# SSM scan of a hybrid decoder layer: chunks stored by their place in the block, a third of the group pairs scanned on GpSimd, queues and order of the work around it changed

## The chip, the cores and the metric

One core of one Trainium2 chip. The metric is the device time of one execution in microseconds (us), median of the runs. Engines: PE = TensorE, DVE = VectorE, ACT = ScalarE, POOL = GpSimd, SP = SyncE (DMA queue only). DMAs are issued from the queues of SP (`dma`), ACT (`put`) and POOL (`later`); each queue is taken in order.

## The reference

One layer for 512 prompt tokens and 8 sample tokens (520 columns), float32:

```
x = x + 0.5 * SwiGLU_1(rmsnorm(x))
z = rmsnorm(x) @ w_in            # [u | q | k | v | gate_a | gate_b]: 1024 + 3*768 + 2*1024 columns
h_t = abar * h_{t-1} + bbar u_t  # S5 SSM: 64 groups of 16 channels, 64 complex states each
y   = gelu(Re(C h) + D u);  A = (y * sigmoid(y @ w_glu)) @ w_proj_a
B   = mixed attention of 3 groups x 4 heads, windows 128/512/2048, dilations 1/4/16, then w_proj_b
x = x + (sigmoid(gate_a) * A + sigmoid(gate_b) * B) @ w_out
x = x + 0.5 * SwiGLU_2(rmsnorm(x))
```

Also returned: the last SSM states, the new keys and values, and the samples' caches moved on by one row.

## The kernel before, in words

Every matrix product is "a product" here: one block of 128 output rows by 520 columns, for K = 1024 eight slices of K, each three matmuls (high x high, high x low, low x high part of a split float32) for each of two column halves: 48 matmuls on line 218 (`mm`). Its weight (512 KB) is loaded by SP (L176), its high part is rounded on ACT (L166), its low part is made on DVE (L167); two raw buffers and six half-weight buffers run ahead. Matmuls under `mark` run on PE in program order.

The mixing stage has 42 products of `w_in` in this order: q blocks 0 and 1; the eight u blocks; q and k blocks 2 to 11; six v blocks; sixteen gates; then eight products of `w_glu`. Behind products the function `pace` counts n (n = 1 behind u block 6, 2 behind u block 7, 3 to 12 behind qk blocks 2 to 11, 13 to 18 behind the v blocks, 19 to 34 behind the gates, 35 on behind `w_glu`) and issues shares of the other work: `SC` scan steps per product, and the lists `LV`, `NB`, `AT`, `KS`, `SM`, `YB` name the n behind which a step of another generator goes.

The SSM path:
- each u block is scaled by 1/rms on DVE into `us` (L791, L793: six instructions), stored to DRAM `uD` by SP (L796, four DMAs a block);
- `entry` (from u block m > `ENTER` = 2 on, four pairs of groups a product): loads of `uD` (POOL, L644) and of the entry matrices `pD` (SP, L658), matmuls on L672, ACT copies into the states `XS` (L673). 32 pairs of groups, 128 chunks of four tokens, plus 8 samples;
- `scan` (L680 to L725), in two halves of 16 pairs on DVE: seven wide steps sum blocks of eight chunks, sixteen short steps carry the state over the sixteen blocks, seven wide steps fill the blocks. `advance` (L688) makes four tensor_tensor instructions: t1 = W0*x, t2 = W1*swap(x), t1 += t2, out = add + t1 (L697 to L700). Chunks lie in the order of time, so a wide step reads and writes every eighth element. The halves are interleaved by `scans`;
- `leave` (L751): eight groups of four pairs; loads of `qD` and `uD` (POOL), 24 matmuls (L758 to L760), one ACT copy (L761), and for each two groups eight stores to `yD` by SP (L768);
- `y_block` (L1037): loads from `yD` (POOL), gelu on ACT and DVE, split; the input of `w_glu`.

Beside it: `normal`/`normalise`/`spread` (norms of q and k, rows broadcast from DRAM `hD` by SP, L844), `attention`, `scores` (samples' scores over the cached keys, in the third buffer of the matrices' ring), `samples`.

Of the kernel before, what the change touches and what calls it, by code (L numbers as in the profile page):

```python
# [10 lines left out]
F32 = mybir.dt.float32  # L11
# [38 lines left out]
SM = (31, 31, 36, 39, 39)  # L50
YB = (29, 29, 29, 29, 29, 31, 31, 33)
NL = 12
# [6 lines left out]
def build(tc, A):  # L59
# [57 lines left out]
    # what is issued inside waits for a value of the arithmetic  # L117
# [5 lines left out]
    # the moves spread over the time of the arithmetic  # L123
# [55 lines left out]
    # the first weights come in halves  # L179
# [25 lines left out]
    # the tensor engine takes these in the order given here  # L205
# [37 lines left out]
    class Norm:  # L243
# [26 lines left out]
        # a quarter of the rows on each quadrant of the partitions while 1/rms is made, then all on each,  # L270
        # through DRAM where that is soon enough
# [33 lines left out]
    def ffn(pf, xs, R, X, last_x, filler, first=(), last=False):  # L305
        first = list(first)

        # products whose rows' 1/rms is still being made leave their banks before it is there
# [14 lines left out]
        for pi, (m0, m1) in enumerate(PARTS):  # L323
# [35 lines left out]
    # the tensor engine's clock rises with use, so it is kept busy while the first rows come  # L359
# [17 lines left out]
    # the first two products go along with the rows' arrival  # L377
# [12 lines left out]
    def ssm_build():  # L390
# [13 lines left out]
        # the skip term joins the lag kernels' first block  # L404
# [56 lines left out]
        # input factor (abar - 1) / lambda  # L461
# [47 lines left out]
        # per eight pairs of groups: entry matrices, exit matrices, lag kernels  # L509
# [5 lines left out]
        for qt in range(4):  # L515
# [15 lines left out]
            # two pairs to a transpose  # L531
# [28 lines left out]
            # a pair to each quarter of the columns  # L560
# [40 lines left out]
    # ================= mixing: one projection, then the SSM and the attention =================  # L601
# [15 lines left out]
    # queries and keys: their 1/rms comes in with the norm over each head  # L617
# [16 lines left out]
    NH = NP // 2  # L634
    XS = [smp.tile([128, 2, NH, 145], F32, name=f"XS{h}") for h in range(2)]
    for ri, n in enumerate(("x0_re", "x0_im")):
        for h in range(2):
            dma(XS[h][:, ri, :, 0:8], A[n].rearrange("p (a b) -> p a b", b=8)[:, h * NH:(h + 1) * NH])
    for h in range(2):
        V.memset(XS[h][:, :, :, 8:9], 0.0)  # L640

# [5 lines left out]
    # block-diagonal over a pair of groups: the blocks are loaded, the zeros stay  # L647
# [16 lines left out]
    # what each chunk's input adds to the state behind it  # L664
    def entry():
        for u in range(NP // 4):
            ut, mp = uload(u), mload(pD, u, dma)
            for a in range(4):
# [4 lines left out]
                S.activation(XS[p // NH][:, :, p % NH, 9:145], ps[:, 0:2], AF.Copy)  # L673
# [4 lines left out]
    # the states in front of every chunk, for a half of the pairs: the sums of sixteen blocks of eight chunks,  # L678
    # the states in front of the blocks, then those inside
    def scan(h):  # L680
        X, pr = XS[h], slice(h * NH, (h + 1) * NH)
        sums = smp.tile([128, 2, NH, 16], F32, name="sums", tag="sums", bufs=2)

# [4 lines left out]
        def advance(out, W, x, add):  # L688
            n = 1 if len(x.shape) == 3 else x.shape[3]
            t1, t2 = (tmp(t)[:, 0:2 * NH * n] for t in "ST")  # L690
            w = [c[:, :, pr] for c in W]
            if n == 1:
                t1, t2 = (t.rearrange("p (r a) -> p r a", r=2) for t in (t1, t2))
            else:
                w = [c.unsqueeze(3).broadcast_to([128, 2, NH, n]) for c in w]
                t1, t2 = (t.rearrange("p (r a b) -> p r a b", r=2, b=n) for t in (t1, t2))
            V.tensor_tensor(t1, w[0], x, ALU.mult)  # L697
            V.tensor_tensor(t2, w[1], swap(x), ALU.mult)  # L698
            V.tensor_tensor(t1, t1, t2, ALU.add)  # L699
            V.tensor_tensor(out, add, t1, ALU.add)  # L700

        def at(j):
            return X[:, :, :, 8 + j:8 + j + 121:8]

        for j in range(1, 8):
            advance(sums, W4, sums if j > 1 else at(1), at(1 + j))
            yield
        for b in range(16):
            advance(X[:, :, :, 16 + 8 * b], W32, X[:, :, :, 8 + 8 * b], sums[:, :, :, b])
# [5 lines left out]
        # sample states  # L715
        x0 = [X[:, ri, :, 0:8] for ri in range(2)]
        xn = [X[:, ri, :, 137:145] for ri in range(2)]
        t = tmp("S")[:, 0:8 * NH].rearrange("p (a b) -> p a b", b=8)
        ab = lambda ri: A1[:, ri, pr].unsqueeze(2).broadcast_to([128, NH, 8])
        for o, a, b, op in ((0, 0, 0, ALU.add), (0, 1, 1, ALU.subtract), (1, 0, 1, ALU.add), (1, 1, 0, ALU.add)):  # L720
            V.tensor_tensor(t, ab(a), x0[b], ALU.mult)
            V.tensor_tensor(xn[o], xn[o], t, op)
        for ri in range(2):
            later(A["ostate"][ri][:, pr], X[:, ri, :, 136:145])
        yield  # L725

    # the short steps of one half go along with the wide ones of the other
    def scans():
        lo, hi = scan(0), scan(1)
        for order in ((lo,) * 7, (lo, hi) * 8, (lo, hi) * 7 + (hi,), (lo,), (hi,) * 8):  # L730
# [3 lines left out]

    scanning = scans()
    paced = {"n": 0, "s": 0}
# [13 lines left out]
    # exit from the states, and the products inside a chunk  # L750
    def leave():  # L751
        for u in range(NP // 4):
            mt, ut, ps = mload(qD, u, later), uload(u), big()
            X, p0 = XS[u * 4 // NH], u * 4 % NH
            for a in range(4):
# [17 lines left out]
    # four segments of tokens, the samples' in front of the first and behind the last, zeros elsewhere;  # L773
    # they go to DRAM with segment and channel on the rows, two groups to a pair
# [3 lines left out]
    for m in range(KB):  # L778
        ps = big()
        mm(ps, wnext(), n2.xs, between=entering if m > ENTER else None)  # L780
        u = us.next()
        # the columns' halves of 260 tokens cut the third segment
        for hf, c0, c1 in ((0, 0, 256), (0, 256, 260), (1, 260, 384), (1, 384, 512)):
            o = u[:, c0 // 128:(c1 + 127) // 128, 8 + c0 % 128:8 + (c1 - 1) % 128 + 1]
            src = ps[:, hf, c0 - hf * H:c1 - hf * H]
            r = R2[:, c0:c1]
            if c1 - c0 > 128:
                src, r = (x.rearrange("p (a b) -> p a b", b=128) for x in (src, r))
            else:
                o = o[:, 0]  # L790
            V.tensor_tensor(o, src, r, ALU.mult)  # L791
        for o in (u[:, 0, 0:8], u[:, 3, NC:CW]):
            V.tensor_tensor(o, ps[:, 1, 512 - H:520 - H], R2[:, 512:520], ALU.mult)  # L793
# [6 lines left out]
    # 1/rms of the rows along the partitions, in the order of the tiles and in that of all the rest  # L800
# [553 lines left out]
```

## Time and profile before

| | us |
|---|---|
| runs (3) | 1324.02, 1325.77, 1328.04 |
| median | 1325.77 |
| span of the profiled execution (first to last instruction) | 1323.7 |
| PE busy | 1265.4 (96%) |
| DVE / ACT / POOL busy | 755.1 / 468.4 / 126.7 |
| mean granted clock of PE | 0.981 |

The profiled execution is one of its own; beside the span lies some 2 us to the median of the runs. Times in views are us from the first instruction. A group row of the trace has its count after "x", then busy us and mean ns of one; after the second bar, idle time in front of the group and what ended it. A window row has, after the stretch and its length, the busy us and count of each engine, the granted clock (PEclk), the busy share of the 16 DMA engines and GB/s.

### The profile page before, as it was taken

What the parts mean: (1) busy time and instruction counts of PE and PEld (TensorE: products, weight loads), DVE (VectorE), ACT (ScalarE), POOL (GpSimd) and SP (SyncE); (2) the same over time, 40 slices, a digit from 0 to 9 for tenths busy, and PEclk for the clock granted to TensorE, in tenths of its full rate; (3) what the DMA queues carried; (4) which work ended last, traced back from release to release, by engine and by line L of the source; (5) the groups of instructions that cost most, each with busy time, mean ns of one, the idle gap of its engine ahead of it and who ended that gap; (6) DMA issues with size and microseconds to landing.
All of it is one profiled execution on the core that took longest, in us unless ns stands there. A gap on an engine that the chain in (4) does not pass through costs nothing.

```text
span 1323.7 us, 25773 instructions
## 1 busy us (share of the span) xinstructions
PE 1265.4 (96%) x10575; PEld 1240.9 (94%) x10575; DVE 755.1 (57%) x1468; ACT 468.4 (35%) x873; POOL 126.7 (10%) x211
## 2 busy tenths in 40 slices
PE   8999999999999779997679999999999999999999
PEld 7999999999999778997578899999999999999998
DVE  6794454545564239999724776776554334444442
ACT  5332233223353223342224564444333223322331
POOL 0120010001103001001221120000010001000000
PEclk9999999999999898998789999999999999999999
DMA  6665366456656445227998635546575436533332
GB/s 216 216 212 178 101 228 191 137 168 206 188 175 155 125 125 155 81 70 242 159 160 245 208 124 145 173 153 206 172 252 162 147 93 223 160 96 112 120 100 85
DMA packets 105438, 213.92 MB, mean 162 GB/s; under 512 B 45300, under 2 KB 61200, under 8 KB 104552
## 3 DMA queue, kind: packets, MB, share of 16 engines
q1 hardware_dynamic: 87064, 145.90, 36.4%
q0 software_dynamic: 7248, 60.01, 15.2%
q10 hardware_dynamic: 11008, 6.36, 2.1%
q8 instruction: 83, 1.36, 0.4%
q14 instruction: 35, 0.29, 0.1%
HBM read 188.72 MB, written 68.60 MB: 194 GB/s over the span
## 4 chain that ended last, share of the span: by engine, by line
PE 76%; DMA 11%; DVE 8%; issue 2%; SPq 1%; ACT 1%; POOL 0%; DVEq 0%; ACTq 0%; POOLq 0%
PE bigB L218 33%; PE bigA L218 28%; PE third L218 12%; DMA wr<-in_win 3%; DMA OB<-hD 2%; DVE wl L167 2%; DMA yD<-XS 2%; DMA t_G<-yD 1%; DVE t_T L698 1%; DVE t_S L697 1%; DMA mt<-qkD 1%; DMA uD<-us 1%; DVE XS L700 1%; DVE t_S L699 1%; ACT wh L166 0%
## 5 line engine op out<-in xcount | busy, mean ns | idle before, releaser
L166 ACT ACTIVATE wh<-wr 128x512 fp32r<-128x512 f32 (+2 forms) x412 | 252.7, 617 | 600.0 <-PE bigB L218 226.0
L167 DVE TENSOR_TENSOR wl<-wr,wh 128x512 fp32r<-128x512 f32 (+2 forms) x412 | 276.6, 672 | 279.6 <-ACT wh L166 275.6
L218 PE MATMUL bigB<-xh,wh 128*128 128x260 f32 (+1 forms) x1216 | 252.9, 289 | 0.3 <-ACT ks L568 0.3
L218 PE MATMUL bigB<-xh,wl 128*128 128x260 f32 (+1 forms) x1216 | 251.9, 287 | 0.0
L218 PE MATMUL bigB<-xl,wh 128*128 128x260 f32 (+1 forms) x1216 | 249.1, 286 | 0.0
L218 PEld LDWEIGHTS bigB<-xh,wl 128*128 128x128 f32 x1216 | 191.6, 191 | 2.4 <-issue 2.4
L218 PEld LDWEIGHTS bigB<-xh,wh 128*128 128x128 f32 x1216 | 190.6, 192 | 1.8 <-issue 0.8
L218 PEld LDWEIGHTS bigB<-xl,wh 128*128 128x128 f32 x1216 | 190.4, 191 | 1.1 <-issue 1.1
L218 PE MATMUL bigA<-xh,wh 128*128 128x260 f32 x704 | 143.1, 284 | 2.5 <-ACT xh L254 2.0
L218 PE MATMUL bigA<-xl,wh 128*128 128x260 f32 x704 | 142.5, 284 | 1.0 <-DVE xl L255 0.9
L218 PE MATMUL bigA<-xh,wl 128*128 128x260 f32 x704 | 142.3, 284 | 0.0
L218 PEld LDWEIGHTS bigA<-xh,wh 128*128 128x128 f32 x704 | 109.1, 190 | 4.4 <-ACT xh L254 3.4
L218 PEld LDWEIGHTS bigA<-xl,wh 128*128 128x128 f32 x704 | 108.8, 189 | 1.6 <-DVE xl L255 1.6
L218 PEld LDWEIGHTS bigA<-xh,wl 128*128 128x128 f32 x704 | 109.1, 190 | 0.2 <-DVE wl L167 0.2
L120 POOL COPY pace<-ah 1x1 f32<-1x1 f32 x48 | 36.1, 751 | 758.2 <-ACT ah L298 758.2
L218 PE MATMUL bigA<-ah,wh 128*128 128x260 f32 x352 | 71.4, 284 | 0.0
L218 PE MATMUL bigA<-al,wh 128*128 128x260 f32 x352 | 71.1, 283 | 0.0
L218 PE MATMUL bigA<-ah,wl 128*128 128x260 f32 x352 | 70.6, 282 | 0.0
L218 PE MATMUL third<-xh,wl 128*128 128x260 f32 x288 | 58.2, 283 | 0.0
L218 PE MATMUL third<-xh,wh 128*128 128x260 f32 x288 | 58.0, 282 | 0.0
L218 PE MATMUL third<-xl,wh 128*128 128x260 f32 x288 | 57.8, 282 | 0.0
L218 PEld LDWEIGHTS bigA<-ah,wh 128*128 128x128 f32 x352 | 54.2, 189 | 0.2
(384 smaller groups left out, 2038.7 us busy)
## 6 DMA issues: line engine op xcount, KB each, us to landing
out_okv<-in_kv POOLq DMA_DIRECT2D x32, 1023.5 KB, 6.3
wr<-in_wg SPq DMA_DIRECT2D x43, 512.0 KB
wr<-in_wu SPq DMA_DIRECT2D x43, 512.0 KB
wr<-in_win SPq DMA_DIRECT2D x42, 512.0 KB
wr<-in_wd SPq DMA_DIRECT2D x32, 448.0 KB
wr<-in_wd SPq DMA_DIRECT2D x16, 512.0 KB
out_okv<-in_kv POOLq DMA_DIRECT2D x8, 1022.0 KB, 5.8
ut<-uD POOLq DMA_DIRECT2D x16, 288.0 KB, 5.5
```

What stands on the lines that cost most here:

```text
L120: ins = G.tensor_copy(pace[0:1, 0:1], t[0:1, 0:1])
L166: S.activation(h, raw, AF.Copy)
L167: V.tensor_tensor(l, raw, h, ALU.subtract)
L218: i = T.matmul(ps[:, hf, 0:x.shape[1]], lhsT=a[:, c], rhs=x, start=k == 0 and j == 0, stop=k == n - 1 and j == 2)
L697: V.tensor_tensor(t1, w[0], x, ALU.mult)
L698: V.tensor_tensor(t2, w[1], swap(x), ALU.mult)
L699: V.tensor_tensor(t1, t1, t2, ALU.add)
L700: V.tensor_tensor(out, add, t1, ALU.add)
```

## The change

It keeps a chunk at column 24 + 16*(place in its block of eight) + block, so that a wide scan step works on runs of 16 adjacent elements; the u blocks are written in that order by DVE and put back in the order of time by the ACT copies of `leave` (three in place of one). The pairs are in three parts (16, 8, 8); the first and the third are scanned on DVE, the second on GpSimd. `sums` and temporaries of a scan are held through it. Queues: `us` stores, `yD` stores and `spread` go from SP to POOL, `pD` loads from SP to ACT, the `Rt` columns and the final states from POOL to SP (the states as six DMAs once at the end). `pace` steps, the lists and `NL` are new; exits come at n = 14 to 18 in place of 21 to 26, y blocks at 25 to 30 in place of 29 to 33, scores at 27 to 31 in place of 22 to 28 with buffers of the samples' ring.

```diff
-ENTER = 2
+ENTER = 3
-SC = 1.85
-LV = (21, 22, 22, 24, 25, 25, 26, 26)
-NB = (16, 17, 17, 17, 18, 18, 19, 20, 21, 22, 22, 22, 22)
-AT = (23, 24, 26, 27, 27, 28, 28, 29, 29, 30, 30, 31, 31, 31, 32, 32, 33, 35, 37)
-KS = (22, 23, 23, 24, 26, 26, 27, 28)
-YB = (29, 29, 29, 29, 29, 31, 31, 33)
-NL = 12
+GROUPS = (16, 8, 8)
+SC = 3.0
+SG = 2.3
+LV = (14, 14, 15, 15, 16, 16, 18, 18)
+NB = (15, 15, 16, 16, 17, 17, 18, 18, 19, 19, 20, 20, 21)
+AT = (22, 23, 24, 24, 25, 25, 26, 27, 27, 28, 28, 29, 30, 30, 31, 32, 32, 33, 35)
+KS = (27, 28, 28, 29, 29, 30, 31, 31)
+YB = (25, 25, 26, 26, 27, 28, 29, 30)
+NL = 6
...
-    XS = [smp.tile([128, 2, NH, 145], F32, name=f"XS{h}") for h in range(2)]
+    XS = [smp.tile([128, 2, n, 160], F32, name=f"XS{h}") for h, n in enumerate(GROUPS)]
...
-            ut, mp = uload(u), mload(pD, u, dma)
+            ut, mp = uload(u), mload(pD, u, put)
...
-    def scan(h):
+    def scan(h, E, tags):
...
-            V.tensor_tensor(t1, w[0], x, ALU.mult)
-            V.tensor_tensor(t2, w[1], swap(x), ALU.mult)
-            V.tensor_tensor(t1, t1, t2, ALU.add)
-            V.tensor_tensor(out, add, t1, ALU.add)
+            E.tensor_tensor(t1, w[0], x, ALU.mult)
+            E.tensor_tensor(t2, w[1], swap(x), ALU.mult)
+            E.tensor_tensor(t1, t1, t2, ALU.add)
+            E.tensor_tensor(out, add, t1, ALU.add)
         def at(j):
-            return X[:, :, :, 8 + j:8 + j + 121:8]
+            return X[:, :, :, 8 + 16 * j:24 + 16 * j]
...
-        lo, hi = scan(0), scan(1)
-        for order in ((lo,) * 7, (lo, hi) * 8, (lo, hi) * 7 + (hi,), (lo,), (hi,) * 8):
+        lo, hi = (scan(h, V, [tmp("G"), tmp("S"), tmp("T")]) for h in (0, 2))
+        for order in ((lo,) * 11, (lo, hi) * 12, (hi,) * 11):
...
+    scanning_too = scan(1, G, [room[:, 1792:2048], dist[:, 0:256], dist[:, 256:512]])
...
-        while paced["s"] < paced["n"] * SC:
+        while paced["s"] < (paced["n"] - 1) * SC:
             next(scanning, None)
             paced["s"] += 1
+        while paced["g"] < (paced["n"] - 3) * SG:
+            next(scanning_too, None)
+            paced["g"] += 1
...
-            S.activation(X[:, 0, p0:p0 + 4, 0:NC].rearrange("p (x a) b -> p x a b", x=2),
-                         ps[:, :, 0:2 * NC].rearrange("p x (a b) -> p x a b", b=NC), AF.Copy)
+            for x in range(2):
+                o, r = X[:, 0, p0 + 2 * x:p0 + 2 * x + 2, 0:NC], ps[:, x, 0:2 * NC].rearrange("p (a b) -> p a b", b=NC)
+                S.activation(o[:, :, 8:NC].rearrange("p a (b j) -> p a b j", j=8),
+                             r[:, :, 8:NC].rearrange("p a (j b) -> p a b j", j=8), AF.Copy)
+            S.activation(X[:, 0, p0:p0 + 4, 0:8].rearrange("p (x a) b -> p x a b", x=2),
+                         ps[:, :, 0:2 * NC].rearrange("p x (a b) -> p x a b", b=NC)[:, :, :, 0:8], AF.Copy)
...
-                        dma(yD[p:p + 8, g2, :, t].rearrange("a k j -> k a j"), X[r0:r0 + 16, 0, p0 - 4:p0 + 4, 0:NC])
+                        later(yD[p:p + 8, g2, :, t].rearrange("a k j -> k a j"), X[r0:r0 + 16, 0, p0 - 4:p0 + 4, 0:NC])
...
+        for sg in range(4):
+            V.tensor_tensor(u[:, sg, 8:NC].rearrange("p (j b) -> p b j", j=8),
+                            *(x.rearrange("p (b j) -> p b j", j=8) for x in
+                              (ps[:, sg // 2, sg % 2 * 128:sg % 2 * 128 + 128], R2[:, sg * 128:sg * 128 + 128])), ALU.mult)
...
-            dma(bass.AP(tensor=o.tensor, offset=o.offset + s * 16 * 4 * CW, ap=[[64 * 4 * CW, 2], [CW, 64], [1, CW]]), u[:, s])
+            later(bass.AP(tensor=o.tensor, offset=o.offset + s * 16 * 4 * CW, ap=[[64 * 4 * CW, 2], [CW, 64], [1, CW]]), u[:, s])
...
-            dma(norms[b % 2][x * 64:x * 64 + 64], hD[2 * b + x:2 * b + x + 1].broadcast_to([64, NT]))
+            later(norms[b % 2][x * 64:x * 64 + 64], hD[2 * b + x:2 * b + x + 1].broadcast_to([64, NT]))
...
-            kt, qb = spare[:, 0:768], spare[:, 768:1536]
+            kt, qb = (sap.tile([128, 768], F32, name="kvt", tag="kvt", bufs=KV) for _ in range(2))
```

## Rows read from the trace of the kernel before

**Rows 1.** The page: the span, and TensorE's busy time, share and instructions.

```profile
span 1323.7 us, 25773 instructions
PE 1265.4 (96%) x10575; PEld 1240.9 (94%) x10575; DVE 755.1 (57%) x1468; ACT 468.4 (35%) x873; POOL 126.7 (10%) x211
```

**Rows 2.** Windows of four stretches, matmuls of L218 on TensorE alone.

```profile
398.20:518.10 119.90, 88.58 (x627) 0.93 0.52 140
518.10:600.00 81.90, 78.68 (x633) 1.00 0.32 94
600.00:700.20 100.20, 44.77 (x331) 0.85 0.90 187
700.20:837.30 137.10, 104.83 (x818) 1.00 0.59 181
```

**Rows 3.** Windows: all engines (PE, PEld, DVE, ACT, POOL) in the first two stretches.

```profile
398.20:518.10 119.90, 102.22 (x803) 98.44 (x804) 52.28 (x131) 32.52 (x71) 17.03 (x27) 0.93 0.52 140
518.10:600.00 81.90, 81.90 (x717) 79.13 (x715) 79.87 (x212) 31.24 (x66) 5.17 (x9) 1.00 0.32 94
```

**Rows 4.** The chain that ended last: start, length, what.

```profile
440.83 0.46 PE s L672 x4
...
664.84 19.65 DMA t_G<-yD
...
1251.56 11.49 PE bigB L218 x96
```

**Rows 5.** Who waited for whom, 390 to 850: PE, then ACT.

```profile
PE bigB L758 <- DMA mt<-qD: 9.6, 1, 9.6
PE s L880 <- DVE OB L921: 6.4, 1, 6.4
...
ACT wh L166 <- DMA wr<-in_win: 81.4, 17, 7.6
ACT t_T L1043 <- DMA t_G<-yD: 14.2, 2, 12.2
```

**Rows 6.** Timeline of the SP queue during the u blocks.

```profile
446.84 6.74 SPq L796 DMA_DIRECT2D uD<-us  x4
453.67 2.47 SPq L176 DMA_DIRECT2D wr<-in_win  x1
```

**Rows 7.** Groups by line and form on DVE, 398 to 720.

```profile
L699 DVE TENSOR_TENSOR t_S<-t_S,t_T 128x512 f32<-128x512 f32 x28 | 19.2, 686 | 0.2
L697 DVE TENSOR_TENSOR t_S<-W,XS 128x512 f32<-128x512 f32 x16 | 18.2, 1136 | 0.1
...
L697 DVE TENSOR_TENSOR t_S<-W,sums 128x512 f32<-128x512 f32 x12 | 8.2, 684 | 0.1
...
L700 DVE TENSOR_TENSOR XS<-sums,t_S 128x32 f32<-128x32 f32 x32 | 6.8, 214 | 0.4
...
L791 DVE TENSOR_TENSOR us<-bigB,R 128x256 f32<-128x256 f32 x8 | 3.3, 417 | 1.6 <-PE bigB L218 1.6
```

**Rows 8.** Timeline of DVE: two independent instructions of a wide step, back to back.

```profile
495.64 0.68 DVE L697 TENSOR_TENSOR t_S<-W,sums 128x512 f32<-128x512 f32 x1
496.24 0.68 DVE L698 TENSOR_TENSOR t_T<-W,sums 128x512 f32<-128x512 f32 x1
```

**Rows 9.** Timeline of POOL's one-element copies, and of DVE beside the last.

```profile
188.33 3.14 POOL L120 COPY pace<-ah 1x1 f32<-1x1 f32 x1 [11.30 <-ACT ah L298]
...
537.83 0.21 POOL L120 COPY pace<-qk 1x1 f32<-1x1 f32 x1 [17.47 <-ACT qk L622]
...
989.88 0.70 DVE L299 TENSOR_TENSOR al<-t_T,ah 128x520 fp32r<-128x520 f32 x1 [0.70 <-ACT ah L298]
989.97 0.64 POOL L120 COPY pace<-ah 1x1 f32<-1x1 f32 x1 [7.56 <-ACT ah L298]
```

**Rows 10.** Groups by line and form on POOL, whole span.

```profile
L658 POOL DMA_DIRECT2D mt<-qD x16 | 12.2, 768 | 32.0 <-PE bigB L760 18.5 <-PE s L672 11.0 <-DMA out_ostate<-XS 1.9
...
L514 POOL MEMSET bpr<- 128x256 f32 x1 | 0.3, 302 | 0.0
```

More of the change, by code (lines that the diff above doesn't have):

```diff
@@ L633, in build, with place @@
     smp = pool(ssm, "smp")
-    NH = NP // 2
-    XS = [smp.tile([128, 2, NH, 145], F32, name=f"XS{h}") for h in range(2)]
+    starts = [sum(GROUPS[:h]) for h in range(3)]
+    XS = [smp.tile([128, 2, n, 160], F32, name=f"XS{h}") for h, n in enumerate(GROUPS)]
     for ri, n in enumerate(("x0_re", "x0_im")):
-        for h in range(2):
-            dma(XS[h][:, ri, :, 0:8], A[n].rearrange("p (a b) -> p a b", b=8)[:, h * NH:(h + 1) * NH])
-    for h in range(2):
+        for h in range(3):
+            dma(XS[h][:, ri, :, 0:8], A[n].rearrange("p (a b) -> p a b", b=8)[:, starts[h]:starts[h] + GROUPS[h]])
+    for h in range(3):
         V.memset(XS[h][:, :, :, 8:9], 0.0)
+    def place(p):
+        h = max(i for i in range(3) if starts[i] <= p)
+        return XS[h], p - starts[h]
     def uload(u):
@@ L672, in entry @@
                     mark(T.matmul(ps[:, ri], lhsT=mp[:, a * 2 + ri], rhs=ut[:, a, 8:CW], start=True, stop=True))
-                S.activation(XS[p // NH][:, :, p % NH, 9:145], ps[:, 0:2], AF.Copy)
+                X, i = place(p)
+                S.activation(X[:, :, i, 24:160], ps[:, 0:2], AF.Copy)
                 yield
     entering = entry()
-    def scan(h):
-        X, pr = XS[h], slice(h * NH, (h + 1) * NH)
-        sums = smp.tile([128, 2, NH, 16], F32, name="sums", tag="sums", bufs=2)
+    def scan(h, E, tags):
+        X, n, pr = XS[h], GROUPS[h], slice(starts[h], starts[h] + GROUPS[h])
+        sums, u1, u2 = (t[:, 0:32 * n].rearrange("p (r a b) -> p r a b", r=2, b=16) for t in tags)
         def swap(x):
@@ L716, in scan, with states @@
         x0 = [X[:, ri, :, 0:8] for ri in range(2)]
-        xn = [X[:, ri, :, 137:145] for ri in range(2)]
-        t = tmp("S")[:, 0:8 * NH].rearrange("p (a b) -> p a b", b=8)
-        ab = lambda ri: A1[:, ri, pr].unsqueeze(2).broadcast_to([128, NH, 8])
+        xn = [X[:, ri, :, 152:160] for ri in range(2)]
+        t = u1.rearrange("p r a b -> p (r a b)")[:, 0:8 * n].rearrange("p (a b) -> p a b", b=8)
+        ab = lambda ri: A1[:, ri, pr].unsqueeze(2).broadcast_to([128, n, 8])
         for o, a, b, op in ((0, 0, 0, ALU.add), (0, 1, 1, ALU.subtract), (1, 0, 1, ALU.add), (1, 1, 0, ALU.add)):
[L721 to L724, printed above, removed]
+            E.tensor_tensor(t, ab(a), x0[b], ALU.mult)
+            E.tensor_tensor(xn[o], xn[o], t, op)
         yield
+    def states():
+        for h in range(3):
+            for ri in range(2):
+                dma(A["ostate"][ri][:, starts[h]:starts[h] + GROUPS[h]], XS[h][:, ri, :, 151:160])
     def scans():
-        lo, hi = scan(0), scan(1)
-        for order in ((lo,) * 7, (lo, hi) * 8, (lo, hi) * 7 + (hi,), (lo,), (hi,) * 8):
+        lo, hi = (scan(h, V, [tmp("G"), tmp("S"), tmp("T")]) for h in (0, 2))
+        for order in ((lo,) * 11, (lo, hi) * 12, (hi,) * 11):
             for x in order:
@@ L753, in leave @@
             mt, ut, ps = mload(qD, u, later), uload(u), big()
-            X, p0 = XS[u * 4 // NH], u * 4 % NH
+            X, p0 = place(u * 4)
             for a in range(4):
@@ L779, in build @@
         ps = big()
-        mm(ps, wnext(), n2.xs, between=entering if m > ENTER else None)
+        mm(ps, wnext(), n2.xs, cut=256, between=entering if m > ENTER else None)
         u = us.next()
[L783 to L791, printed above, removed]
+        for sg in range(4):
+            V.tensor_tensor(u[:, sg, 8:NC].rearrange("p (j b) -> p b j", j=8),
+                            *(x.rearrange("p (b j) -> p b j", j=8) for x in
+                              (ps[:, sg // 2, sg % 2 * 128:sg % 2 * 128 + 128], R2[:, sg * 128:sg * 128 + 128])), ALU.mult)
         for o in (u[:, 0, 0:8], u[:, 3, NC:CW]):
-            V.tensor_tensor(o, ps[:, 1, 512 - H:520 - H], R2[:, 512:520], ALU.mult)
+            V.tensor_tensor(o, ps[:, 1, 256:264], R2[:, 512:520], ALU.mult)
         for s in range(4):
             o = uD[m]
-            dma(bass.AP(tensor=o.tensor, offset=o.offset + s * 16 * 4 * CW, ap=[[64 * 4 * CW, 2], [CW, 64], [1, CW]]), u[:, s])
+            later(bass.AP(tensor=o.tensor, offset=o.offset + s * 16 * 4 * CW, ap=[[64 * 4 * CW, 2], [CW, 64], [1, CW]]), u[:, s])
         if m > 5:
@@ L810, in build @@
         if b == RB:
-            with behind(qk[b]):
-                columns()
+            columns()
         pace()
@@ L925, in build @@
     later(A["ovt"].rearrange("r p f -> p r f"), vt)
-    dist = atp.tile([128, 512], F32, name="dist")
     dma(dist, A["dist"])
@@ L1151, in build @@
     side.append((list(AT), attending))
-    side.append((list(KS), scores()))
-    side.append((list(SM), samples()))
     yout = outputs()
@@ L1157, in build @@
         if i == NL:
-            assert not side[0][0] and next(scanning, None) is None and not side[3][0]
+            assert not side[0][0] and next(scanning, None) is None and next(scanning_too, None) is None
+            states()
             ssm.close()
@@ L1163, in build @@
             sap = pool(saps, "sap")
+            side.append((list(KS), scores()))
+            side.append((list(SM), samples()))
             side.append((list(YB), yout))
```

29 lines of the change are left out of this document (14 added, 15 removed).

## The prediction

> **What bounds the kernel now.** First the page: TensorE is busy 96% of a span of 1323.7 us [rows 1], so a change of the SSM's course can only give back what TensorE loses around it. Next the chain that ended last: undisturbed, 96 matmuls of L218 take 11.49 us [rows 4], 0.1197 us each, so a product of 48 takes 5.75 us. Then windows over the mixing, to see where the products run slower than that. They are cut at the last entry matmul (518.1), at 600, at the end of the worst stretch (700.2) and at the end of the `w_glu` products (837.3).
>
> - 398.2 to 518.1, u blocks and entry: 627 matmuls are worth 75.1 us [rows 2]; entry puts 0.46 us a pair [rows 4] on TensorE, 32 x 0.46 = 14.7; the small products on norms some 2. That is 92 of 119.9 us: **28 us lost**.
> - 518.1 to 600: 633 x 0.1197 = 75.8 of 81.9 [rows 2], the rest is other matmuls: about 2 lost. But DVE is busy 79.87 of 81.9 [rows 3]: the scan has it to itself here.
> - 600 to 700.2: 331 x 0.1197 = 39.6; I estimate the exits and the first attention at 22: **39 us lost**. The granted clock is 0.85 of full speed here and DMA busy 0.90 [rows 2].
> - 700.2 to 837.3: 97.9 of products, some 31 of attention, exits and samples: about 8 lost.
>
> So 77 us are there to be won. Who ends the waits: in the first stretch ACT waits 81.4 us for weights [rows 5], because SP, which loads them, spends 6.74 us on four `us` stores between two weights [rows 6], and the entry's PSUM copies sit behind ACT's wait. In the third, TensorE waits 9.6 us for an exit matrix and 6.4 us for a value block's samples that DVE scales late, behind the scan; and ACT is held 12.2 us by a `yD` load [rows 5], which took 19.65 us to come [rows 4].
>
> **The change part by part.**
>
> *Queues in the u blocks.* 32 `us` stores of 1.69 us (6.74/4 [rows 6]) and 16 `pD` loads leave SP: 54 us and more of a queue that has a weight to issue every 7.6 us. On POOL I take the 0.77 us that a matrix load costs to issue [rows 10], 32 x 0.77 = 25 us, and POOL is busy only 17 of 120 us here [rows 3]; its `uD` loads wait behind the stores, which they need anyway. ACT is busy 32.5 of 119.9 [rows 3] and takes the 16 loads; they wait for a matrix buffer freed three groups earlier, so nothing behind them (weight rounding) should be held. ENTER = 3 gives stores and loads one product more. The six DVE instructions of a block become four strided and two short ones: a strided 512 costs 1136 in place of 684 ns [rows 7], so at worst eight blocks cost 0.7 us more each, in DVE's idle 56%; without that cover TensorE would wait for a bank. I leave 8 us of the 28 lost (bounds 3, as in the second stretch, and 28, nothing gained).
>
> *Wide steps on adjacent elements.* An instruction that reads or writes every eighth element takes 1136 ns, one on adjacent ones 684 to 686 [rows 7]. Before, a wide step is 4 instructions, of 28 steps: 32 strided reads and 28 strided writes at 1.136, 52 others at 0.685: 104 us, and 32 short steps 4 x 0.21 x 32 = 27: 131 us in all on DVE. After, all wide ones take the short price. Back to back they start 0.60 us apart [rows 8], so a 16-pair step costs 2.6 us with its two dependent starts, an 8-pair step 1.5 (417 ns for 256 elements [rows 7], less the same overlap). First part: 14 x 2.6 + 16 x 0.7 + 2 = 49.5; third: 14 x 1.5 + 16 x 0.65 = 31.5.
>
> *The GpSimd part.* 56 wide and 72 short instructions. No row shows a two-operand instruction on POOL. From below: a memset of 256 elements takes 0.302 us [rows 10], a one-element copy 0.21 [rows 9]: 32 us. From above: two operands as two passes, 0.60: 49 us. I take 45, nearer to two passes because each operand must be read. What it shares with DVE decides more. The same copy takes 0.64 us when DVE starts a tensor_tensor of two SBUF operands 0.09 us before it, and 3.14 us in front of a run of them [rows 9]: POOL waits until DVE leaves a gap. Whether DVE in turn waits for a running POOL instruction no row shows; between nothing and all of the 45 us I take all, since whoever holds what they share held it to its end in these rows. The Trainium skill (SBUF — State Buffer, section "Who interferes with whom") says so of both sides: a DVE instruction with two SBUF inputs and a GpSimd one that reads SBUF exclude each other, and the second to issue stands still. By that rule the two sums add up; by these rows alone only POOL's is stretched. It speaks against this change.
>
> *When the scans end.* Their first 16 pairs are entered when the tenth product ends: 398.2 + 57.5 + 16 x 0.46 + 2 = 465, with part of the 8 us 469. From there until the exits are served DVE has 49.5 + 31.5 of scan, 18 products' two low halves (36 x 0.60 = 22), and about 10 of norms that must go between: 113 us. With POOL's 45 that is 627; some 5% of DVE's time is idle or on PSUM operands, so I take **620**. Without any wait TensorE would ask for the first exit (n = 14) at 398.2 + 22 x 5.75 + 14.7 + 6.5 of small products + 8 = 554 and for the GpSimd part's (n = 16) two products and four exit groups of 2.8 us later, at 577. So TensorE waits some 45 us here, in place of the 39 of before: what is late next is the GpSimd part.
>
> *From there to the end.* Before, 17 products lie behind 700.2 (818/48 [rows 2]). Behind the fifth exit group 26 are left, nine more, and four exit groups where 49/24 = two are left before: 137.1 + 9 x 5.75 + 2 x 2.8 + 5 (attention done before 700.2) = 199.5 us, with the 8 us lost there kept. 620 + 199.5 = 819.5 against 837.3: **18 us sooner**; 638 is the point from which the change is slower.
>
> *Moved onto POOL behind its scan:* 32 `yD` stores, 24 `spread`, the remaining `qD` loads: 68 x 0.77 = 52 us of issue [rows 10] in the order of the queue. Norms of q and k are due by n = 22, six products and the exits later, so most is covered; I put nothing on the sum and 8 on the upper bound. SP gets five short loads and six state stores, all behind weights that run ahead: nothing. ACT's exits, three instructions for one: 4 us over a stage in which it is 30% busy: nothing. y blocks four products earlier, scores in ring buffers: TensorE loses only 8 us there now; the wait of ACT for a `yD` load may come again (12.2 us [rows 5]), or vanish: -5 to +12 for the range. The split of u columns at 256 keeps the count of matmuls.
>
> **Sum.** The profiled execution ends 18 us sooner by its span of 1323.7; the median of the runs is 2 us above that span, and the same lies around it after: 1325.8 - 18 = **1308**. A measurement of this kernel tells about 0.3% (4 us) from no change.
>
> **The rivals.**
>
> *POOL is starved (slower), 0.20.* It decides from 638 on. DVE's scan is nearly without gaps (79.87 of 81.9 [rows 3]), and a single copy waited 3.14 us before it [rows 9]. If POOL gets in only when DVE runs dry, at 469 + 113 + 8 = 590, its 45 to 49 us end near 640, and the `spread` DMAs behind it hold the first attention some 10 us more: 650 + 199.5 = 849.5, **1338**. For it: those copies. Against it: each wide step has two dependent starts, at which DVE leaves a gap, and the copy at 537.83, amid the scan, took 0.21 [rows 9].
>
> *DVE does not pay for POOL, 0.22.* Then the first part is done at 469 + 49.5 + 16.5 of the third's steps + 18 + 3.5 = 556, when it is asked for, POOL by about 580, and TensorE has next to no wait: 579 + 199.5 = 778.5, with 5 for POOL's queue 783: **1272**. For it: no DVE row is lengthened by a POOL copy. Against: those copies are the shortest there are.
>
> *The first stretch is not freed, 0.08.* If the stores are as slow from POOL and the entry waits for them, 20 of the 28 us stay and all behind comes as much later: **1328**.
>
> *The layout doesn't do what it says, 0.05.* If the broadcast weights and not the step of eight made 1136 ns, the scans grow by 23 us: 643, **1331**. Against: the same weights with `sums` take 684 [rows 7].
>
> **How the numbers follow.** The forecast has 0.45; its own range is 1293 to 1322 (first stretch 3 to 15 us lost, POOL 32 to 49 us). The range for 8 in 10 takes in the second rival's price and most of the first's: 1272 to 1342. Faster by over 0.3%: 0.41 of the forecast's 0.45 and the 0.22: 0.63. Within 0.3%: 0.04, the unfreed stretch and part of the layout's: 0.13. Slower: 0.24.
>
> **What would show it.** In the windows of after: the u blocks' stretch some 20 us shorter, no 6 us of stores between weights on SP. Wide L697 to L700 of 512 elements near 685 ns; of 256 on DVE near 420. POOL's instructions of the scan well over their bare price, and DVE's sum of scan rows under 90 us but with gaps or lengthened instructions where POOL runs. TensorE's longest wait in front of exit matmuls, released by POOL's scan, ending near 620. I am wrong if that wait ends after 638, if it is missing, or if TensorE waits again at 700 to 837 (attention, y blocks) for DMAs that POOL issued late.

## The result and the profile after

The changed kernel takes 1337.4 us (median of 4 runs, 1336.1 to 1337.9) against 1326.9 us before in the same comparison (4 runs): a ratio of 1.0076, 95% interval 1.0055 to 1.0097. It is slower by some 10 us; 18 us faster was forecast. The profiled execution has a span of 1335.2 us against 1323.7 [rows 1].

The page of the changed kernel, its span and busy times:

```profile
span 1335.2 us, 25915 instructions
PE 1264.6 (95%) x10575; PEld 1241.2 (93%) x10575; DVE 747.1 (56%) x1469; ACT 473.0 (35%) x889; POOL 250.9 (19%) x417
```

POOL's busy time doubled (126.7 before [rows 1]); TensorE's work is the same, so the 11 us are waits or low clock. The windows, product matmuls alone (L221, which was L218), cut at the last entry matmul (502.7), at 600, at the end of the worst stretch (665) and at the end of the `w_glu` products (848.8); columns as in [rows 2]:

```profile
398.20:502.70 104.50, 90.90 (x665) 0.97 0.63 157
502.70:600.00 97.30, 55.55 (x432) 0.88 0.45 75
600.00:665.00 65.00, 19.00 (x132) 0.71 0.84 176
665.00:848.80 183.80, 150.96 (x1169) 1.00 0.58 180
```

The first stretch came out as forecast: entry ends at 502.4 in place of 517.7, and with the prediction's own prices (665 x 0.1197 + 14.7 + 2 = 96.3 of 104.5) 8.2 us are lost there, where it left 8. The last stretch runs at full clock without gaps. Nearly all the rest is lost between 519 and 665. Who ends TensorE's waits from 500 to 665 (total, times, longest):

```profile
PE sb L963 <- ACT qk L912: 25.2, 1, 25.2
PE bigB L778 <- issue: 16.7, 1, 16.7
PE bigB L780 <- DMA ut<-uD: 6.3, 1, 6.3
PE sb L630 <- ACT t_sq L628: 5.2, 2, 4.8
PE sb L963 <- DVE qk L867: 3.8, 1, 3.8
```

4.8 us at 519, where ACT is late because it waited 11.35 us for a weight; 16.7 us in front of the first exit (it starts at 577.1, just behind DVE's last wide instruction of the first part); 6.3 us for a block of u inside an exit; and 25.2 + 3.8 us in front of the first attention matmuls (they start at 644.7), which want normalised queries and keys. The wait of 25.2 us is the longest, and the prediction had no such wait. The wait behind GpSimd's scan, which the prediction made the longest, is not in the list. Behind each of the waits from 4.8 us up TensorE runs for some us at the lower of its two clock levels (1.2 in place of 2.4 GHz). The timeline of PE after the 16.7 us:

```profile
577.66 0.66 PE L779 MATMUL bigB<-XS,mt 128*128 128x136 f32 x2
578.12 0.66 PE L780 MATMUL bigB<-ut,mt 128*128 128x136 f32 x2
...
583.30 0.39 PE L779 MATMUL bigB<-XS,mt 128*128 128x136 f32 x2
583.53 0.40 PE L780 MATMUL bigB<-ut,mt 128*128 128x136 f32 x2
```

Two exit matmuls start 0.46 us apart first and 0.23 us some 5 us later. That is part of why the granted clock reads 0.88 from 502.7 to 600; behind the later waits the same comes again, and it reads 0.71 from 600 to 665.

The scan's rows, 398 to 665, DVE's then POOL's (DVE's had 684 to 686 ns for 512 adjacent elements and 214 for 32 before [rows 7]):

```profile
L707 DVE TENSOR_TENSOR t_S<-t_S,t_T 128x512 f32<-128x512 f32 x14 | 11.7, 835 | 0.2
L706 DVE TENSOR_TENSOR t_T<-W,XS 128x512 f32<-128x512 f32 x8 | 7.5, 942 | 0.0
...
L705 DVE TENSOR_TENSOR t_S<-W,XS 128x32 f32<-128x32 f32 x16 | 6.0, 373 | 0.2
...
L708 POOL TENSOR_TENSOR XS<-XS,dist 128x256 f32<-128x256 f32 x8 | 8.2, 1022 | 0.5
```

All of POOL's scan rows sum to 79.2 us (45 were counted), and DVE's rows grew as well. A piece of the timeline where both scan, with instructions of both at about 1.1 us (start, length):

```profile
556.08 1.16 POOL L706 TENSOR_TENSOR dist<-W,XS 128x256 f32<-128x256 f32 x1
...
556.68 1.11 DVE L707 TENSOR_TENSOR t_S<-t_S,t_T 128x512 f32<-128x512 f32 x1
...
557.32 1.06 POOL L707 TENSOR_TENSOR dist<-dist 128x256 f32<-128x256 f32 x1
```

Last, the DMA view of 570 to 600 us, where the norms go to DRAM and the exits' matrices come (line, engine, count, KB each, median us from issue to landing):

```profile
DMA packets 4732, 2.32 MB, mean 77 GB/s; under 512 B 4222, under 2 KB 4222, under 8 KB 4729
...
mt<-qD POOLq DMA_DIRECT2D x4, 192.0 KB, 15.4
ut<-uD POOLq DMA_DIRECT2D x2, 288.0 KB, 15.0
...
out_ostate<-XS SPq DMA_DIRECT2D x2, 72.0 KB, 15.1
```

The state stores write nine floats, 36 bytes, a run. Nearly all packets are that small, and the engines move little in a window in which the exits' loads and the state stores take 15 us to land.

### The profile page after: what moved, and what is told of

It is laid out like the page before. It is cut to its first block, busy times and chain, and to the rows that moved or that the text cites. A ratio compares the mean times of both kernels' runs of the same rounds, so it can differ in the third digit from the quotient of the medians.

```text
span 1335.2 us, 25915 instructions
## 1 busy us (share of the span) xinstructions
PE 1264.6 (95%) x10575; PEld 1241.2 (93%) x10575; DVE 747.1 (56%) x1469; ACT 473.0 (35%) x889; POOL 250.9 (19%) x417
## 4 chain that ended last, share of the span: by engine, by line
PE 79%; DVE 8%; DMA 7%; issue 2%; POOL 2%; SPq 1%; ACT 0%; ACTq 0%; POOLq 0%; DVEq 0%
PE bigB L221 36%; PE bigA L221 28%; PE third L221 12%; DMA uD<-us 2%; DVE t_S L707 2%; DVE t_T L706 2%; DVE wl L170 2%; DMA OB<-hD 1%; DVE t_S L705 1%; DVE XS L708 1%; DMA hD<-nq 1%; PE s L992 1%; PE sb L963 1%; DMA kvt<-qkD 1%; DMA kvt<-in_kv 1%
## 5 line engine op out<-in xcount | busy, mean ns | idle before, releaser
L170 DVE TENSOR_TENSOR wl<-wr,wh 128x512 fp32r<-128x512 f32 (+2 forms) x412 | 279.7, 679 | 286.8 <-ACT wh L169 274.4
L221 PE MATMUL bigB<-xh,wh 128*128 128x260 f32 (+1 forms) x1216 | 254.1, 289 | 1.9 <-ACT XS L786 1.7
L221 PE MATMUL bigB<-xh,wl 128*128 128x260 f32 (+1 forms) x1216 | 250.5, 286 | 0.0
L221 PE MATMUL bigB<-xl,wh 128*128 128x260 f32 (+1 forms) x1216 | 249.5, 286 | 0.0
L221 PEld LDWEIGHTS bigB<-xh,wh 128*128 128x128 f32 x1216 | 190.9, 192 | 4.3 <-ACT XS L786 1.9
L221 PEld LDWEIGHTS bigB<-xh,wl 128*128 128x128 f32 x1216 | 190.5, 191 | 1.8 <-issue 1.8
L221 PEld LDWEIGHTS bigB<-xl,wh 128*128 128x128 f32 x1216 | 190.3, 191 | 1.7 <-issue 1.3
L221 PE MATMUL bigA<-xh,wh 128*128 128x260 f32 x704 | 143.1, 284 | 1.4 <-ACT xh L257 1.4
L221 PE MATMUL bigA<-xl,wh 128*128 128x260 f32 x704 | 142.5, 284 | 0.5 <-DVE xl L258 0.4
L221 PE MATMUL bigA<-xh,wl 128*128 128x260 f32 x704 | 142.0, 283 | 0.0
L221 PEld LDWEIGHTS bigA<-xh,wh 128*128 128x128 f32 x704 | 109.1, 190 | 3.5 <-ACT xh L257 3.1
L221 PEld LDWEIGHTS bigA<-xl,wh 128*128 128x128 f32 x704 | 108.6, 189 | 1.6 <-DVE xl L258 1.6
L221 PEld LDWEIGHTS bigA<-xh,wl 128*128 128x128 f32 x704 | 108.9, 189 | 0.0
L221 PE MATMUL bigA<-ah,wh 128*128 128x260 f32 x352 | 71.4, 284 | 0.0
L221 PE MATMUL bigA<-al,wh 128*128 128x260 f32 x352 | 71.1, 283 | 0.0
L221 PE MATMUL bigA<-ah,wl 128*128 128x260 f32 x352 | 70.6, 282 | 0.0
L221 PE MATMUL third<-xh,wl 128*128 128x260 f32 x288 | 58.2, 283 | 0.0
L221 PE MATMUL third<-xh,wh 128*128 128x260 f32 x288 | 58.0, 282 | 0.0
L221 PE MATMUL third<-xl,wh 128*128 128x260 f32 x288 | 57.8, 282 | 0.0
L221 PEld LDWEIGHTS bigA<-ah,wh 128*128 128x128 f32 x352 | 54.2, 189 | 0.2
```

The source lines that it names most:

```text
L170: V.tensor_tensor(l, raw, h, ALU.subtract)
L221: i = T.matmul(ps[:, hf, 0:x.shape[1]], lhsT=a[:, c], rhs=x, start=k == 0 and j == 0, stop=k == n - 1 and j == 2)
```

## The experiments

Times are medians, ratios are to runs of the kernel before on the same chip, with 95% intervals. A difference between two kernels is that of their ratios, in us of 1326.

### 1. Broadcasts of the norms back on SP

```
-            later(norms[b % 2]..., hD[...].broadcast_to([64, NT]))
+            dma(norms[b % 2]..., hD[...].broadcast_to([64, NT]))
```

> The changed kernel with one thing put back: the 24 broadcast loads of the norms (OB<-hD) are issued from SP again and no longer from POOL, behind its scan. Three theories stand. THEORY SHARING: GpSimd's scan and DVE's exclude each other (POOL's scan rows sum to 79 us, DVE's 128x512 additions take 835 ns in place of 686), so the scans end late and that is the whole loss; this edit is then worth under 4 us, 1333 to 1341 us. THEORY NORMS' QUEUE: the longest wait of TensorE (25.2 us before the first attention matmul) comes from broadcasts that stand in POOL's queue behind yD stores, loads for the y blocks and the tail of the scan; issued from SP they go as soon as their buffers come free, the last some 10 to 18 us sooner, the wait falls to 8 to 15 us, and the kernel takes 1320 to 1329 us. THEORY SMALL STORES: the 36-byte runs of the state stores crowd the DMA engines from 580 us on, hD lands 13 us after its issue, and the broadcasts are late whoever issues them; under 4 us gained, and each broadcast still takes some 10 us to land.

1338.3 us, 1.0105 (1.0079 to 1.0131): nothing won. The longest wait before the attention is still 21.3 us. The broadcasts of this run, by their line (count; first and last start):

```profile
L861 SPq DMA_DIRECT2D OB<-hD x24: 444/565/661, 598.8 to 637.2; - x24
...
DMA to landing us min/median/max: 2.9/4.6/11.6
```

They begin at 598.8, 12 us after the last of the norms' own stores (586.4), and the longest took 11.6 us to land (the median 4.6): what they carry comes late, whoever issues them. Still they came sooner: the last starts at 637.2 in place of 652.6, and the first attention matmul at 628.6 in place of 644.7. It won nothing because the next product starts at 652.4, as in the changed kernel (651.8). In both it needs ACT's copy out of an exit, which waits for the steps of GpSimd's scan that make the samples' states. ACT and TensorE (start, length, idle time and its releaser), the changed kernel, then this one:

```profile
651.55 0.28 ACT L786 ACTIVATE XS<-bigB 128x32 f32<-128x32 f32 x2 [6.88 <-POOL dist L730]
651.80 0.80 PE L221 MATMUL bigB<-xh,wh 128*128 128x260 f32 x2 [1.65 <-ACT XS L786]
```

```profile
652.10 0.28 ACT L786 ACTIVATE XS<-bigB 128x32 f32<-128x32 f32 x2 [2.08 <-POOL dist L730]
652.35 0.80 PE L221 MATMUL bigB<-xh,wh 128*128 128x260 f32 x2 [7.09 <-ACT XS L786]
```

So two limits end at nearly the same time there, the norms and GpSimd's last steps. The broadcasts' place in POOL's queue alone is not the cause, and that part of my theory fell; the queue as a whole this run doesn't clear.

### 2. The second part scanned by DVE

```
-    scanning_too = scan(1, G, [...])
+    scanning_too = scan(1, V, [...])
```

> The changed kernel with its second part (8 pairs) scanned by DVE and not by GpSimd; places, order and queues stay. SHARING: DVE's instructions go back to 686 ns (512 elements) and 417 (256), the second part costs it some 31 us in place of the 79 us of POOL that it had to stand aside for, the first exit is served some 10 us sooner or at the same time and all parts by 605 us in place of 613; 10 to 20 us gained, 1318 to 1328 us. NORMS' QUEUE: the scan's tail leaves POOL's queue, which helps the broadcasts by a few us; 1330 to 1336 us. SMALL STORES: the stores still crowd the broadcasts; 1333 to 1341 us.

1308.7 us, 0.9882 (0.9858 to 0.9907): 26 us below the changed kernel, more than the theory of sharing expected. DVE's rows are back near their short price:

```profile
L707 DVE TENSOR_TENSOR t_S<-t_S,t_T 128x512 f32<-128x512 f32 x14 | 9.8, 701 | 0.1
...
L706 DVE TENSOR_TENSOR t_T<-W,XS 128x512 f32<-128x512 f32 x8 | 5.7, 712 | 0.0
```

All scan rows on DVE sum to 136.2 us here, against 117.8 for its two parts in the changed kernel: giving 8 of the 32 pairs to GpSimd, for 79.2 us there, freed DVE of 18. The broadcasts and the norms' stores in front of them (min/median/max ns, first and last start), the changed kernel first, then this one:

```profile
L861 POOL DMA_DIRECT2D OB<-hD x24: 522/528/555, 604.5 to 652.6; - x24
L844 SPq DMA_DIRECT2D hD<-nq x4: 355/364/6822, 583.0 to 590.7; - x4
```

```profile
L861 POOL DMA_DIRECT2D OB<-hD x24: 516/538/566, 566.7 to 665.1; - x24
L844 SPq DMA_DIRECT2D hD<-nq x4: 333/351/366, 563.6 to 564.8; - x4
```

DVE computes the norms between steps of the scan, and finishes them some 20 us sooner. In the changed kernel the last matmuls that they need start at 551.5 and DVE turns to the norms only at 569.2; here it is 539.6 and 540.7. The wait before the attention is gone. What is left in 500 to 665 is the first exit's wait and the blocks of u:

```profile
PE bigB L778 <- DVE XS L708: 15.7, 1, 15.7
PE bigB L780 <- DMA ut<-uD: 11.5, 5, 9.2
```

### 3. Nobody scans the second part

```
-        V.memset(XS[h][:, :, :, 8:9], 0.0)
+        V.memset(XS[h][:, :, :, 8:24], 0.0)
-            next(scanning_too, None)
+            pass
```

> The changed kernel without the scan of its second part: nobody computes it, the places of the states of these 8 pairs hold zeros and the outputs that hang on them are not computed. So it shows what GpSimd's scan costs as a whole, to whomever. SHARING: DVE's rows take their bare durations, the first exit is served where it is asked for (560 us), and most of the 48 us that TensorE waits between 550 and 660 us goes: 1295 to 1310 us. NORMS' QUEUE: the wait before the exit goes, but the one before the attention grows by part of it, since the broadcasts still queue behind yD stores and loads: 1315 to 1325 us. SMALL STORES: the states are stored sooner too, and still in front of hD's broadcasts: 1320 to 1330 us.

1290.3 us, 0.9735 (0.9713 to 0.9758): 45 us below the changed kernel. DVE's 512-element rows are at 685 to 691 ns, its two parts sum to 92.1 us in place of 117.8, and the first exit starts at 549. That is below the ranges of all three theories. Scanned by DVE the second part costs 19 us (0.9882 against 0.9735), scanned by GpSimd 45, of which DVE's longer rows are 25.7.

### 4. No state stores

```
-                dma(A["ostate"][ri][:, starts[h]:...], XS[h][:, ri, :, 151:160])
+                if h == 0 and ri == 0:
+                    dma(A["ostate"][ri][:, 0:1], XS[h][:, ri, 0:1, 151:160])
```

> The changed kernel without its state stores, but for one column of one part: the states that are an output are not stored; nothing that is computed changes. SMALL STORES: with the 36-byte runs gone hD lands 3 to 5 us after its issue in place of 13, the uD blocks for the exits come in time (6.3 us of TensorE's waits go), the norms are done some 10 us sooner; 10 to 18 us gained, 1320 to 1328 us. SHARING and NORMS' QUEUE: under 5 us gained, 1332 to 1341 us.

1318.0 us, 0.9941 (0.9922 to 0.9961): 18 us below the changed kernel, just under the range for small stores, with GpSimd's scan in place. The wait for a block of u is gone, the first broadcast starts at 588.7 in place of 604.5, and the long wait before the attention falls from 25.2 to 18.7 us. The small stores are a second cause.

### 5. Complete kernel, states stored packed

```
+        o = so[:, ...].rearrange("p (r a b) -> p r a b", r=2, b=9)
+        E.tensor_copy(o, X[:, :, :, 151:160])
+        for ri in range(2):
+            dma(A["ostate"][ri][:, pr], o[:, ri])
...
-            states()
```

> The changed kernel, complete, GpSimd scanning its part; each part's nine states a pair are first copied side by side into a tile of their own by the engine that scanned it, and stored from there at the end of its scan, in runs of 576 or 288 bytes in place of 36. SMALL STORES: the gain of leaving the stores out (1338 to 1318 us) comes back almost whole, hD lands within 6 us of its issue: 1317 to 1325 us. SHARING alone: what the run without stores won came from SP's order (the norms' stores no longer behind stores that wait) or from somewhere else; then the packed stores still stand in SP's queue and win under half of it: 1328 to 1340 us.

1318.1 us, 0.9905 (0.9882 to 0.9928): as good as no stores at all, 23 us below the changed kernel. The DMA view of the same 30 us:

```profile
DMA packets 2107, 5.57 MB, mean 186 GB/s; under 512 B 493, under 2 KB 845, under 8 KB 2103
...
mt<-qD POOLq DMA_DIRECT2D x8, 192.0 KB, 5.0
ut<-uD POOLq DMA_DIRECT2D x4, 288.0 KB, 5.4
...
out_ostate<-so SPq DMA_DIRECT2D x2, 72.0 KB, 1.6
```

The same 72 KB land in 1.6 us in place of 15.1, and loads beside them in 5 in place of 15: 2.4 times the bytes are moved. The first two stores start at 579.6, as before (579.9), and still stand in front of the norms' stores: it was the runs of 36 bytes, not the volume and not this place in SP's queue.

### 6. DVE alone and packed states; then later exits

> The changed kernel, complete, with the second part scanned by DVE and the states stored packed. If SHARING (28 us in the run with DVE alone) and SMALL STORES (19 us in the run without them) are two costs at two places, most of both is gained: 1292 to 1302 us, and the 11.5 us that TensorE waits for uD blocks in the run with DVE alone fall under 4. If they are one cost (the norms late behind the scan, by either way), the packing adds nothing to DVE alone: 1304 to 1311 us.

1290.1 us, 0.9697 (0.9672 to 0.9723): 50 us below the changed kernel, where the two alone won 26 and 23. They are two costs. All engines from 600 to 665 us (PE, PEld, DVE, ACT, POOL, granted clock, DMA share, GB/s), the changed kernel, then this one:

```profile
600.00:665.00 65.00, 33.31 (x240) 32.32 (x239) 23.20 (x56) 13.08 (x35) 39.74 (x75) 0.71 0.84 176
```

```profile
600.00:665.00 65.00, 64.49 (x541) 63.77 (x541) 29.10 (x58) 28.29 (x57) 28.05 (x50) 1.00 0.75 226
```

TensorE does more than twice the matmuls in it and holds its full clock. The one long wait left is the first exit's, 15.7 us, on DVE's scan. So, on top:

```
-LV = (14, 14, 15, 15, 16, 16, 18, 18)
+LV = (17, 17, 18, 18, 19, 19, 20, 20)
```

> As the run before (DVE scans all, states packed), and the exits from the states stand three products and more later in TensorE's order (behind 17, 17, 18, 18, 19, 19, 20, 20 in place of 14 to 18). If the 15.7 us wait before the first exit (DVE's scan of part one not ready) only needs products in front of it, it goes nearly whole: 8 to 14 us below the run before. If the y blocks and what hangs on them (behind 25 to 30 products) come late instead, TensorE waits there for t_G or yD and the gain is under 4 us.

1284.1 us, 0.9659 (0.9631 to 0.9688), 5 us below the run before; the two intervals overlap, so the size is uncertain; it lies between the two expectations. The 15.7 us became 7.7, and 4.6 us before the attention came back:

```profile
PE bigB L785 <- issue: 6.4, 1, 6.4
PE sb L970 <- DVE qk L874: 4.6, 1, 4.6
...
PE bigB L785 <- DVE XS L710: 1.3, 1, 1.3
```

This is the fastest version: 3.4% under the kernel before and 4.1% under the changed one (0.9659 / 1.0076).

### 7. Can GpSimd's part be saved?

GpSimd alone, with the scans on DVE left out:

```
-            next(scanning, None)
+            pass
```

> The changed kernel with GpSimd's scan alone: DVE's scans of parts one and three are left out, the places of their states hold zeros and what hangs on them is not computed. It measures GpSimd's instructions without a scan on DVE beside them (DVE's other work stays). SHARING: the bare durations seen where DVE was between instructions, 0.62 to 0.74 us for 256 elements and 0.23 to 0.30 us for 16, so 56 wide ones at 0.66, 64 short ones at 0.26 and 8 of the samples at 0.3 make some 56 us in place of 79. Against it: GpSimd is as slow by itself; its wide rows stay at 0.77 to 1.02 us and the sum near 79 us, and only DVE's longer rows are a price of sharing.

One run (1309.7 us, of an incomplete kernel). GpSimd's rows without a scan beside them:

```profile
L707 POOL TENSOR_TENSOR dist<-dist 128x256 f32<-128x256 f32 x14 | 13.5, 964 | 1.0
...
L706 POOL TENSOR_TENSOR dist<-W,XS 128x256 f32<-128x256 f32 x8 | 5.1, 641 | 0.0
```

The sum is 65.3 us, between the two expectations: up to 20 us over the 45 that were counted are GpSimd's own price (DVE's other work still ran beside it), 14 more come with DVE's scan. Most rows of 256 elements are at 0.64 to 0.80 us; the addition of two scratch tiles stays at 0.96, and why isn't settled. And with the late exits and packed states that suited DVE alone:

> As the run with DVE alone, packed states and late exits, but GpSimd scans its part. If SHARING costs only where TensorE waits for an exit or for norms, and later exits give cover, GpSimd's scan comes out within 8 us of DVE alone: 1285 to 1293 us. If it holds DVE up as a whole, so that norms, weights' second parts and the scan all come later, most of the 28 us stay: 1303 to 1314 us.

1310.5 us, 0.9891 (0.9862 to 0.9919), 31 us above its twin with DVE alone. Cover in front of the exits doesn't hide it. TensorE waits there 12.6 us for blocks of u inside exits, where its twin waits for none. This pair also rules out that the price is only the standing of the changed kernel's scan behind loads and stores in POOL's queue: here GpSimd's last step comes at 576.7, in the changed kernel at 653.1, and the price is as high.

```profile
576.74 0.35 POOL L733 TENSOR_TENSOR XS<-XS,dist 128x64 f32<-128x64 f32 x1
```

Three pairs of kernels that differ in this one letter (G or V in experiment 2) give 26, 28 and 31 us.

### 8. Parts of it in the kernel before

The queues alone (`us` stores on POOL, `pD` loads on ACT):

```
-            ut, mp = uload(u), mload(pD, u, dma)
+            ut, mp = uload(u), mload(pD, u, put)
...
-            dma(bass.AP(tensor=o.tensor, ...), u[:, s])
+            later(bass.AP(tensor=o.tensor, ...), u[:, s])
```

> The kernel before, with the queues of the u blocks alone: us stores from POOL, pD loads from ACT; entry's matmuls stay where they were (ENTER 2). The prediction put 20 us on the queues in the first stretch. If the scan behind it starts as much sooner and nothing else is late, 1306 to 1316 us. If what comes sooner only waits at the exits and the attention of 600 to 700 us, 1319 to 1327 us.

1321.9 us, 0.9972 (0.9957 to 0.9987): 4 us. Packed states alone (the copy as in 5, on DVE):

> The kernel before, with its states copied side by side by DVE and stored packed, nothing else. SMALL STORES as an old cost: POOL waits 7.55 us and 1.93 us for those stores there, with uD and qD loads behind it, and the DMA engines are busy 0.90 from 600 to 700 us; 1312 to 1321 us. As a cost that the change brought (it put the stores on SP, beside hD's, before the norms): under 4 us gained, 1322 to 1329 us.

1310.7 us, 0.9885 (0.9859 to 0.9911): 15 us. The small stores were an old cost. Both:

> The kernel before with two things: the u blocks' queues (5 us alone) and the packed states (16 us alone). What lies between it and the changed kernel with DVE alone and packed states (1290 us) is the worth of the places, the three parts and the new order together, without GpSimd. If the two gains add up, 1302 to 1309 us, and places and order are worth 12 to 19 us. If with the crowding gone the entry's earlier end is worth the 15 us that the prediction counted, 1292 to 1300 us, and places and order are worth almost nothing beside it. If both gains are the same one, 1309 to 1314 us.

1310.2 us, 0.9883 (0.9840 to 0.9926): the queues add nothing to the packed states that these runs can tell (the interval is 0.9% wide). Windows of the kernel with packed states alone, product matmuls as in [rows 2]:

```profile
518.10:600.00 81.90, 78.45 (x628) 1.00 0.31 94
600.00:700.20 100.20, 53.49 (x403) 0.91 0.81 238
```

Where its 15 us begin: 72 product matmuls more than before fit into 600 to 700 (331 in [rows 2]), 8.6 us of work, at a granted clock of 0.91 for 0.85, with 238 GB/s for 187.

## Why the prediction was wrong

The books of the change, all from pairs of kernels: places, three parts and new order without GpSimd win 25 us (0.9697 against 0.9883, both with the queues and packed states); the queues win 0 to 4; GpSimd loses 26 to 31; and the small stores, which cost 15 before, cost 23 to 25 now, 8 to 10 more. The sum lies between 5 and 16 us lost; 10 were measured.

- **Queues of the u blocks: right in the stretch, worth little behind it.** 8.2 us were lost there, 8 forecast. But alone in the kernel before they brought 6 us at the end of entry (511.3 for 517.7) and 4 at the end. The rest of the 15 us that entry ends sooner came with other parts of the change (one product more of lead, the u blocks' new form); which one wasn't tried.
- **Wide steps: right in kind, not a saving in sum.** A wide instruction of 512 elements takes 685 to 691 ns in experiment 3 and 688 to 712 in experiment 2, for 1136. But DVE's whole scan took 134.3 us by its rows before (129.7 without the samples' steps; the prediction counted 131) and takes 136.2 in the new form of experiment 2: parts of 8 pairs use some 430 ns for half the elements and 215 for 16 in place of 214 for 32. I take it that what pays is the order, which lets TensorE exit from the first part while the others are scanned; no run tried it alone.
- **The GpSimd part: the term that was most under-sized.** "I take 45" measured 65.3 without a scan on DVE and 79.2 beside DVE; the upper bound of 49, two passes of a memset, was too low because no row of that kernel had GpSimd read two operands. "Between nothing and all of the 45 us I take all" was a guess in the right direction: DVE's two parts grew by 25.7 us (92.1 to 117.8). Counted by the prediction's own steps, GpSimd's part cost 45 in place of 31.5 on DVE, 13.5 us; three pairs of kernels say 26 to 31. That is half of the miss. The Trainium skill (SBUF — State Buffer, section "Who interferes with whom") has the two engines share a pair of ports under an exclusive lock; the longer rows on both sides agree with it. Whether it kept the two apart at all times the runs don't show.
- **"When the scans end", 620: near by luck.** POOL's last wide instruction starts at 612.3 and DVE's at 610.9, but not for the reasons counted. POOL had only one wide step of its part left at 571.8. Then its queue stood 11.3 us in front of a load whose buffer the late first exit frees, and 9.3 us in front of a `yD` store; the samples' steps came between norms' broadcasts, up to 653:

```profile
570.73 1.05 POOL L708 TENSOR_TENSOR XS<-XS,dist 128x256 f32<-128x256 f32 x1
583.09 0.60 POOL L653 DMA_DIRECT2D ut<-uD  x1 [11.31 <-PE bigB L780]
...
612.27 0.78 POOL L708 TENSOR_TENSOR XS<-XS,dist 128x256 f32<-128x256 f32 x1
...
653.09 0.33 POOL L731 TENSOR_TENSOR XS<-XS,dist 128x64 f32<-128x64 f32 x1
```

The step took POOL's queue as one that only the scan fills. TensorE's waits at the exits are 16.7 + 6.3 us in place of 45, and the longest was for DVE's first part: the wait behind POOL's scan is missing, by the prediction's own words a sign of being wrong.
- **"From there to the end, 199.5 us": the step that failed.** It took 848.8 - 612 = 237. Attention was taken as behind 620 without a wait of its own. The step's words were "I put nothing on the sum and 8 on the upper bound" for the norms; 25.2 + 3.8 us were waited for them, with the lower clock after. The suspect named there, the broadcasts in POOL's queue, is not the cause by itself: on SP they came sooner and nothing was won, since GpSimd's samples' steps held the next product to the same time (experiment 1). Two things made the norms late. DVE finished them 20 us later than in experiment 2, behind its own longer instructions. And the small stores delayed their way through DRAM: the last of four `hD` stores was issued at 590.7, behind two state stores on SP, and landed 13 us later, as the chain that ended last has it:

```profile
590.66 13.08 DMA hD<-nq
```

- **"Six state stores ... nothing": wrong.** They cost 23 us in the changed kernel. A row said so beforehand: POOL's `mt` load waits for `out_ostate<-XS` [rows 10], and the DMA engines are busy 0.90 in the worst stretch at 187 GB/s [rows 2], where they move 238 at 0.81 once the states are packed. I read the wait (1.9 us) and not the size of the runs.
- **The rivals.** "POOL is starved" gave 1338, and 1337 was measured, but by another way: POOL wasn't kept waiting until DVE ran dry: all but one of its wide steps were done at 571.8, most instructions longer, and what held it after that was its queue. So the near number is luck. "DVE does not pay" is excluded by the rows. The first stretch was freed, and the layout did what it says to a wide instruction.

Open remains how the 26 to 31 us divide between the later norms and the later exits, since both hang on the same longer instructions, and what the places are worth without the three parts; neither was tried alone.

## What to carry to other kernels

Before work is given to GpSimd beside DVE, time one such instruction there with DVE running: 79 us on GpSimd freed DVE of 18, and its other work came later too. And what is put on an engine whose queue also issues DMAs stands behind their waits. Look at the size of runs and not only at bytes: one copy into a tile that makes a store's runs 288 to 576 bytes long in place of 36 was worth 15 us in one kernel and 23 in the other. And when a stage is pulled forward, ask of everything that the next stage wants (norms here) when it will be there, not only of what is moved.

## What was not expected of the hardware

72 KB in runs of 36 bytes took 15.1 us to land, packed 1.6 us, and while they ran, loads of 192 to 288 KB took 15 in place of 5 us. The Trainium skill (DMA: Bandwidth & Descriptors, section "Why small descriptors are slow (HBM only)") gives each descriptor a fixed overhead whatever it carries. 77 against 186 GB/s in the same 30 us point the same way; how much of the difference is that overhead no run here tells. That other queues' transfers are delayed as well is what these runs add. And a two-operand instruction of GpSimd over 256 elements a partition took 641 to 964 ns without a scan on DVE beside it (experiment 7), where a memset of as many took 302 [rows 10].
